# The first two projection chunks of a layer, walked by token halves over eight weight loads

## The chip, the cores and the metric

The kernel runs on one core of a Trainium2 chip. The metric is the device time of one execution in microseconds (us); it is the median of three timed runs. All times inside an execution are read from one profiled run, in us from the start of its span.

## What is computed

The reference is a two-layer decoder trunk over 256 tokens of width 2048. The part that matters here is the start of each layer: a row norm with a gain, and one wide projection whose output columns feed everything behind it.

```
def rms_norm(x, g):
    x32 = x.astype(jnp.float32)
    y = x32 * lax.rsqrt(jnp.mean(x32 * x32, axis=-1, keepdims=True) + EPS)
    return (y * g.astype(jnp.float32)).astype(x.dtype)
...
    u = rms_norm(h, norm_mix_pre)
    proj = u @ w_in
    offsets = tuple(int(o) for o in np.cumsum(IN_SIZES)[:-1])
    (nsa_q, nsa_kv, nsa_g, lru_x, lru_y,
     gla_q, gla_k, gla_v, gla_r, gla_z) = jnp.split(proj, offsets, axis=-1)
```

## The kernel before

Every matrix product is made of split operands: a value is the sum of a rounded part (`hi`, made by a ScalarE cast) and a rest (`lo`, a VectorE subtraction), and three matmuls (hi by hi, hi by lo, lo by hi) give one product. The helper `split` (L147 and L148) makes both parts, for the activations `u` and for every weight tile.

**Weights** come as a list of loads, in the order in which the projections use them (`plan`). `ensure` (L203 on) issues the next load from SyncE into one of four `raw` buffers and records its split into one of eight `hi`/`lo` buffers. A load therefore waits until VectorE has finished the split of the load four places ahead of it, and a split waits until TensorE has finished with the tile eight places ahead. All loads leave from SP's one queue, in the order of the program, and each waits for the load eight places ahead of it to land.

**The first two chunks of a layer** are `vw` (256 columns, four loads of 512 KB, four row blocks each) and `vs` (eight loads of 256 KB, two row blocks each). The tile of a `vs` load has 320 columns: 256 come with the load, the other 64 are gate columns, which lie elsewhere in `w_in`. These 64 are fetched once per layer for all eight tiles by two extra loads (`self.gz`, in `ensure`): 16 and 48 columns for each of 2048 rows, so runs of 64 and 192 bytes. Each `vs` tile then needs a second small split, out of that fetched tile. A `vs` matmul reads all 320 columns.

The 256 tokens are two halves of 128 (`hf`), because the stationary operand holds 128 tokens. Before, `form_a` ran `vw` with all its four loads for half 0 and then for half 1 (`grp=4`), and then `vs` load by load, both halves of each load in turn (`grp=1`). Each chunk has one accumulator per half, and `evac` copies it out behind the last matmul.

**The operand `u`** of the first layer is made in `run`: per half, ScalarE squares the four tiles of `h` with a running sum, VectorE and GpSimd turn that into a row factor, ScalarE scales each tile by it (L163) and VectorE multiplies by the gain (L151). `to_t` then transposes each tile on TensorE (L311) and splits the result. For the second layer the same is done at the end of the first layer, in `ev_pg` and `pre_norm`.

Other loads at the start: the input `x` in eight tiles `h`, the gain in two halves, the constants `cst`, two 512 KB loads of `nsa_cmp_w` (runs of 256 bytes) and nine small ones into `rows` (`load_params`). The order on each engine is set by a scheduler that works on the recorded program; it moves instructions ahead of others where it finds room.

Of the kernel before, what the change touches and what calls it, by code (L numbers as in the profile page):

```python
# [13 lines left out]
AF = mybir.ActivationFunctionType  # L14
ALU = mybir.AluOpType
# [16 lines left out]
NBUF = 8  # L32
# [68 lines left out]
class Trunk:  # L101
# [129 lines left out]
    def form_a(self, base, nu, k0, ut, evac, grp=1, kpu=2, w=512, ring=None):  # L231
        accs = [(ring or self.acc)() for _ in range(2)]
        self.ensure(base)
        for g in range(0, nu, grp):
            us = range(g, min(nu, g + grp))
            for hf in range(2):
                for u in us:
                    self.ensure(base + u)
                    hi, lo = self.loaded[base + u]
                    for k in range(kpu):  # L240
                        kt = k0 + kpu * u + k
                        uh, ul = ut.get(kt, hf * 128, hf * 128 + 128)
                        wh, wl = hi[:, k * w:k * w + w], lo[:, k * w:k * w + w]
                        last = u == nu - 1 and k == kpu - 1
                        o = accs[hf][:, 0:w]
                        self.mm(o, uh, wh, u == 0 and k == 0, False)
                        self.mm(o, uh, wl, False, False)
                        self.mm(o, ul, wh, False, last)
                    if hf:
                        self.ensure(base + u + NBUF)  # L250
                    self.pump(0.72 * kpu * w / 1024)
                if g + grp >= nu:
                    evac(hf, accs[hf])

    def banks(self, which):

        if which == "acc":
            return [self.acc() for _ in range(4)]
        return [self.sc(), self.sc(), self.tr(), self.tr()]
# [176 lines left out]
    def layer(self, i, ut):  # L436
        nc, a = self.nc, self.a
        B = lambda *k: self.base[(i,) + k]
# [5 lines left out]

        v = self.unit().rearrange("p (h b n) -> p h b n", h=2, b=2)

        self.form_a(B("vw"), 4, 0, ut, lambda hf, acc: nc.scalar.copy(v[:, hf, 1], acc[:, 0:256]), 4, 4, 256)
        gt = self.st([P, 2, 48], "gt", 1)
        z = self.sm(32)

# [2 lines left out]
            nc.vector.tensor_copy(z[:, hf * 16:hf * 16 + 16], acc[:, 256:272])  # L453
            self.actf(gt[:, hf], acc[:, 272:320], AF.Tanh, scale=0.5)
        rows = self.load_params(i)
        self.form_a(B("vs"), 8, 0, ut, ev_vs, 1, 2, 320)
        self.ts(gt, gt, 0.5, 0.5)
        gtv = self.st([P, 2, 16], "gtv", 1)
        self.tt(gtv, gt.rearrange("p h (n b) -> p h n b", b=3)[:, :, :, 0],
# [18 lines left out]
        for _ in range(2):  # L478
            t = self.unit(F32R)
            kh.append(t.rearrange("p (g b t) -> p g b t", g=2, b=2))  # L480
            t = self.unit(F32R)
# [101 lines left out]
        gpre = self.gain("norm_mlp_pre", i)  # L583
# [96 lines left out]
        last = i == self.depth - 1  # L680
        ss = [self.sm(4) for _ in range(2)]
        if not last:
            gpre = self.gain("norm_mix_pre", i + 1)
# [422 lines left out]
    def run(self):  # L1106
        self.plan()
        a = self.a
        self.h = [[self.sb.tile([P, 512], F32, name=f"h{hf}{n}") for n in range(4)] for hf in range(2)]
        ut = self.new_ut()  # L1110
        for hf in range(2):
            for n in range(4):
                self.dma(self.h[hf][n], a["x"][0, hf * 128:hf * 128 + 128, n * 512:n * 512 + 512])
            if hf == 0:
                gpre = self.gain("norm_mix_pre", 0)
                self.ensure(1)
            ss = self.sm(4)
            with self.tc.high_priority():
                for n in range(4):
                    self.sumsq(self.h[hf][n], ss[:, n:n + 1])  # L1120
                self.nrm[hf] = self.st([P, 4], "nrm", 4)
                r = self.rstd(ss, keep=self.nrm[hf])
                for n in range(4):
                    t = self.t2()
                    self.actf(t, self.h[hf][n], AF.Copy, scale=r)
                    self.tt(t, t, self.col(gpre, n))
                    self.to_t(t, n, hf, ut)
        self.cst2()
        for i in range(self.depth):
            ut = self.layer(i, ut)  # L1130
# [33 lines left out]
```

## Time and profile before

| | |
|---|---|
| median of three runs | 2487.36 us (2486.42 to 2487.51) |
| profiled execution | 2485.96 us |
| its span, first to last instruction | 2484.2 us, so 1.76 us lie around it |
| TensorE (PE) busy | 2458.3 us, 99% of the span |
| VectorE (DVE) busy | 1527.9 us, 62% |
| ScalarE (ACT) busy | 1279.2 us, 51% |
| mean granted TensorE clock | 0.997 |

The busy share of PE counts the time in which a matmul is under way; the chain that ended last tells what the end of the program waited for, step by step. A timeline row gives the start of a group of equal instructions, its time, and in brackets how long the engine was idle before it and what ended that. PE, DVE, ACT and SPq (the DMA issues of SyncE) have rows of their own, and L166 and L147/L148 are lines of helpers, so the names of the tiles tell which step a row belongs to.

### The profile page before, as it was taken

How to read it: one execution, taken by the hardware profiler on the slowest of the kernel's cores; microseconds unless marked ns; L12 is line 12 of the kernel's file. 1: busy time of each engine (PE TensorE's matmuls, PEld its weight loads, DVE VectorE, ACT ScalarE, POOL GpSimd, SP SyncE). 2: the span in 40 equal slices, each digit the busy share in tenths (PEclk: the TensorE clock that was granted, in tenths of full speed). 3: DMA queues.
4: the chain of work that ended last, by engine and by line, in shares of the span. 5: the costliest groups of instructions: out<-in, count | busy, mean ns of one | idle time of the engine just before them, and what ended most of it. 6: DMA issues, size and time to landing. Idle time of an engine off the chain costs nothing.

```text
span 2484.2 us, 33780 instructions
## 1 busy us (share of the span) xinstructions
PE 2458.3 (99%) x12950; PEld 2079.8 (84%) x12950; DVE 1527.9 (62%) x2098; ACT 1279.2 (51%) x2008; POOL 27.6 (1%) x42
## 2 busy tenths in 40 slices
PE   8999999999999999999999999999999999999999
PEld 7888888888888888888888888888888888888887
DVE  5776767754555554656667767676545546555574
ACT  6676655554443443445456765654544434444452
POOL 0000000000000000000000000000000000000000
PEclk9999999999999999999999999999999999999999
DMA  8644445556656556665575445456566565565653
GB/s 255 196 136 136 150 161 195 184 189 193 191 189 196 189 187 195 189 208 186 188 196 166 130 144 155 161 181 201 189 194 188 190 194 191 188 195 187 210 182 125
DMA packets 286371, 452.20 MB, mean 182 GB/s; under 512 B 32984, under 2 KB 107744, under 8 KB 286208
## 3 DMA queue, kind: packets, MB, share of 16 engines
q1 hardware_dynamic: 286208, 450.03, 56.9%
q8 instruction: 102, 1.67, 0.3%
q14 instruction: 61, 0.50, 0.1%
HBM read 447.88 MB, written 2.10 MB: 181 GB/s over the span
## 4 chain that ended last, share of the span: by engine, by line
PE 93%; DVE 3%; ACT 1%; DMA 1%; issue 1%; POOL 0%; DVEq 0%; ACTq 0%; SPq 0%; POOLq 0%
PE acc L166 62%; PE tr L166 14%; PE sc L166 14%; PE tr L873 1%; DMA raw<-in_w_up_dram 1%; DVE lo L148 1%; ACT t L163 1%; ACT hi L147 0%; PE tr L311 0%; DVE h L154 0%; DVE t L154 0%; DVE u L148 0%; DVE u L151 0%; POOL sm L301 0%; DVE u L154 0%
## 5 line engine op out<-in xcount | busy, mean ns | idle before, releaser
L148 DVE TENSOR_TENSOR lo<-raw,hi 128x1024 fp32r<-128x1024 f32 (+1 forms) x832 | 1007.2, 1213 | 789.9 <-ACT hi L147 784.8
L147 ACT CAST hi<-raw 128x1024 fp32r<-128x1024 f32 (+1 forms) x832 | 865.9, 1043 | 982.1 <-PE acc L166 571.8
L166 PE MATMUL acc<-hi,u 128*128 128x512 f32 (+2 forms) x2944 | 900.4, 384 | 3.7 <-DVE u L148 1.4
L166 PEld LDWEIGHTS acc<-hi,u 128*128 128x128 f32 x2944 | 547.2, 189 | 109.9 <-ACT u L147 2.5
L166 PE MATMUL acc<-lo,u 128*128 128x512 f32 (+2 forms) x1472 | 563.8, 383 | 0.9 <-DVE lo L148 0.9
L166 PE MATMUL acc<-u,hi 128*128 128x512 f32 x1920 | 490.2, 395 | 0.0
L166 PEld LDWEIGHTS acc<-u,hi 128*128 128x128 f32 x1920 | 344.6, 189 | 65.5 <-issue 3.1
L166 PEld LDWEIGHTS acc<-lo,u 128*128 128x128 f32 x1472 | 277.6, 189 | 52.4 <-DVE lo L148 1.4
L166 PEld LDWEIGHTS acc<-u,lo 128*128 128x128 f32 x1920 | 262.0, 190 | 18.9
L166 PE MATMUL acc<-u,lo 128*128 128x256 f32 x1920 | 268.2, 282 | 0.0
L166 PE MATMUL sc<-u,hi 128*128 128x512 f32 x512 | 140.3, 394 | 0.0
L166 PE MATMUL tr<-u,hi 128*128 128x512 f32 x512 | 138.4, 391 | 0.0
L166 PE MATMUL sc<-hi,u 128*128 128x512 f32 x384 | 119.3, 389 | 0.0
L166 PE MATMUL tr<-hi,u 128*128 128x512 f32 x384 | 119.2, 389 | 0.0
L166 PEld LDWEIGHTS tr<-u,hi 128*128 128x128 f32 x512 | 95.6, 188 | 21.5 <-issue 0.8
L166 PEld LDWEIGHTS sc<-u,hi 128*128 128x128 f32 x512 | 88.5, 190 | 11.8
L166 PEld LDWEIGHTS sc<-u,lo 128*128 128x128 f32 x512 | 78.3, 189 | 10.0
L166 PEld LDWEIGHTS tr<-hi,u 128*128 128x128 f32 x384 | 72.1, 188 | 14.9
L166 PEld LDWEIGHTS sc<-hi,u 128*128 128x128 f32 x384 | 72.1, 188 | 14.8
L166 PE MATMUL tr<-u,lo 128*128 128x256 f32 x512 | 82.9, 283 | 0.0
L166 PE MATMUL sc<-u,lo 128*128 128x256 f32 x512 | 81.3, 282 | 0.0
L166 PE MATMUL sc<-lo,u 128*128 128x512 f32 x192 | 74.8, 389 | 0.0
(185 smaller groups left out, 1705.6 us busy)
## 6 DMA issues: line engine op xcount, KB each, us to landing
raw<-in_w_up_dram SPq DMA_DIRECT2D x256, 512.0 KB, 3.7
raw<-in_w_down_dram SPq DMA_DIRECT2D x256, 512.0 KB, 3.5
raw<-in_w_in_dram SPq DMA_DIRECT2D x168, 512.0 KB, 3.7
raw<-in_w_out_dram SPq DMA_DIRECT2D x64, 512.0 KB, 3.6
raw<-in_w_ple_gate_dram SPq DMA_DIRECT2D x64, 512.0 KB, 4.1
raw<-in_w_in_dram SPq DMA_DIRECT2D x16, 256.0 KB, 3.0
raw<-in_w_ple_dram SPq DMA_DIRECT2D x8, 512.0 KB, 3.4
h<-in_x_dram SPq DMA_DIRECT2D x8, 256.0 KB
```

Of the source, the lines that this page charges most:

```text
L147: self.nc.scalar.copy(hi, src)
L148: self.nc.vector.tensor_sub(lo, src, hi.bitcast(F32))
L163: self.nc.scalar.activation(out, a, f, **k)
L166: self.nc.tensor.matmul(out, l, r, start=start, stop=stop, skip_group_check=True)
L873: nc.tensor.transpose(b[:, x * 128:x * 128 + 128], pe[:, x * 128:x * 128 + 128], self.ident)
```

## The change

The body of `form_a`'s innermost loop becomes a function of its own, `a_unit`. In `layer`, the two calls of `form_a` for `vw` and `vs` are replaced by one loop: first half 0 over the four `vw` loads and the first four `vs` loads, then half 1 over the same eight, then half 0 and half 1 over the last four `vs` loads. Four accumulators are taken at once. `load_params` now stands ahead of both chunks. In `run`, the scaling on ScalarE and the gain product on VectorE become one VectorE instruction, `stt` (L154, scalar_tensor_tensor).

```diff
@@ form_a @@
             for hf in range(2):
                 for u in us:
-                    self.ensure(base + u)
-                    hi, lo = self.loaded[base + u]
...
-                    if hf:
-                        self.ensure(base + u + NBUF)
-                    self.pump(0.72 * kpu * w / 1024)
+                    self.a_unit(base, u, nu, kpu, w, k0, ut, hf, accs[hf])
                 if g + grp >= nu:
                     evac(hf, accs[hf])
+
+    def a_unit(self, base, u, nu, kpu, w, k0, ut, hf, acc):
+        self.ensure(base + u)
+        hi, lo = self.loaded[base + u]
+        o = acc[:, 0:w]
+        for k in range(kpu):
+            kt = k0 + kpu * u + k
+            uh, ul = ut.get(kt, hf * 128, hf * 128 + 128)
+            wh, wl = hi[:, k * w:k * w + w], lo[:, k * w:k * w + w]
+            last = u == nu - 1 and k == kpu - 1
+            self.mm(o, uh, wh, u == 0 and k == 0, False)
+            self.mm(o, uh, wl, False, False)
+            self.mm(o, ul, wh, False, last)
+        if hf:
+            self.ensure(base + u + NBUF)
+        self.pump(0.72 * kpu * w / 1024)
@@ layer @@
-        self.form_a(B("vw"), 4, 0, ut, lambda hf, acc: nc.scalar.copy(v[:, hf, 1], acc[:, 0:256]), 4, 4, 256)
...
         rows = self.load_params(i)
-        self.form_a(B("vs"), 8, 0, ut, ev_vs, 1, 2, 320)
+
+        jobs = []
+        for key, nu, kpu, w, ev in (("vw", 4, 4, 256, lambda hf, acc: nc.scalar.copy(v[:, hf, 1], acc[:, 0:256])),
+                                    ("vs", 8, 2, 320, ev_vs)):
+            jobs.append((B(key), nu, kpu, w, ev, [self.acc() for _ in range(2)]))
+        self.ensure(B("vw"))
+        for part in ((0, 0, 4), (1, 0, 4)), ((1, 4, 8),):
+            for hf in range(2):
+                for x, u0, u1 in part:
+                    base, nu, kpu, w, ev, accs = jobs[x]
+                    for u in range(u0, u1):
+                        self.a_unit(base, u, nu, kpu, w, 0, ut, hf, accs[hf])
+                    if u1 == nu:
+                        ev(hf, accs[hf])
@@ run @@
                     t = self.t2()
-                    self.actf(t, self.h[hf][n], AF.Copy, scale=r)
-                    self.tt(t, t, self.col(gpre, n))
+                    self.stt(t, self.h[hf][n], r, self.col(gpre, n), op0=ALU.mult, op1=ALU.mult)
                     self.to_t(t, n, hf, ut)
```

Beyond the starts of the two layers the order of the instructions is the same on every engine. Three places show what moved.

SP's queue in the first layer, behind the fourteen loads that both kernels begin with (`raw_268` and `raw_286` are the last two `vw` loads, `raw_317` on are `vs` loads, `u_321` is the tile of the gate columns). Before:

```order
L144 DMA raw_268<-in_w_in_dram 128x4x256 [waits DMAHW6_49]
L144 DMA raw_286<-in_w_in_dram 128x4x256 [waits DMAHW7_49]
L144 DMA raw_317<-in_w_in_dram 128x2x256 [waits DMAHW0_49,DVE_49]
L144 DMA raw_328<-in_w_in_dram 128x2x256 [waits DMAHW1_49,DVE_49]
L144 DMA rows_423<-in_lru_conv_w_dram 16x128 [waits DMAHW2_49]
L144 DMA rows_423<-in_lru_conv_b_dram 4x128 [waits DMAHW3_49]
L144 DMA rows_423<-in_lru_ba_dram 4x128 [waits DMAHW4_49]
L144 DMA u_237<-in_nsa_cmp_w_dram 128x16x64 [waits DMAHW5_49]
L144 DMA u_238<-in_nsa_cmp_w_dram 128x16x64 [waits DMAHW6_49]
L144 DMA u_321<-in_w_in_dram 128x16x16 [waits DMAHW7_49]
L144 DMA u_321<-in_w_in_dram 128x16x48 [waits DMAHW0_49]
L144 DMA raw_336<-in_w_in_dram 128x2x256 [waits DMAHW1_49,DVE_49]
```

Now, behind the same fourteen and nine `rows` loads (`raw_274` and `raw_292` are the last two `vw` loads, `raw_311` on are `vs` loads, `u_315` takes the gate columns; DMAHW0 to DMAHW7 are the eight places of which each load waits for its own, DVE is a wait for a split):

```order
L144 DMA raw_274<-in_w_in_dram 128x4x256 [waits DMAHW7_49]
L144 DMA u_229<-in_nsa_cmp_w_dram 128x16x64 [waits DMAHW0_49]
L144 DMA u_230<-in_nsa_cmp_w_dram 128x16x64 [waits DMAHW1_49]
L144 DMA raw_292<-in_w_in_dram 128x4x256 [waits DMAHW2_49]
L144 DMA raw_311<-in_w_in_dram 128x2x256 [waits DMAHW3_49,DVE_49]
L144 DMA raw_328<-in_w_in_dram 128x2x256 [waits DMAHW4_49,DVE_49]
L144 DMA raw_342<-in_w_in_dram 128x2x256 [waits DMAHW7_49,DMAHW5_49,DVE_49]
L144 DMA raw_356<-in_w_in_dram 128x2x256 [waits DMAHW6_49,DMAHW2_49,DVE_49]
L144 DMA raw_382<-in_w_in_dram 128x2x256 [waits DMAHW3_49,DVE_49]
L144 DMA raw_402<-in_w_in_dram 128x2x256 [waits DMAHW4_49,DMAHW0_49,DVE_49]
L144 DMA u_315<-in_w_in_dram 128x16x16 [waits DMAHW1_49]
L144 DMA u_315<-in_w_in_dram 128x16x48
```

All nine `rows` loads and both `nsa_cmp_w` loads now stand ahead of the fourth `vw` load, and the gate columns stand behind six `vs` loads instead of two, four of which wait for splits of this stage.

PE's queue where `vs` begins in the first layer. Before (`acc_243` is `vw` for half 1, `acc_433` and `acc_434` are `vs` for half 0 and half 1):

```order
L166 MATMUL acc_243<-lo_288,u_85 128x256
L166 MATMUL acc_243<-hi_287,u_85 128x256
L166 MATMUL acc_433<-hi_318,u_78 128x320 [waits Activation_49]
L166 MATMUL acc_434<-hi_318,u_78 128x320
L166 MATMUL acc_433<-lo_319,u_78 128x320 [waits DVE_49]
```

Now (`acc_246` is `vw` for half 0, `acc_248` is `vs` for half 0):

```order
L166 MATMUL acc_246<-lo_294,u_85 128x256
L166 MATMUL acc_246<-hi_293,u_85 128x256
L166 MATMUL acc_248<-hi_312,u_78 128x320 [waits Activation_49]
L166 MATMUL acc_248<-lo_313,u_78 128x320 [waits DVE_49]
L166 MATMUL acc_248<-hi_312,u_78 128x320 x2
L166 MATMUL acc_248<-lo_313,u_78 128x320
```

Half 1 of `vw`, 48 matmuls, stood ahead of the first `vs` matmul and now stands behind the 24 matmuls of half 0 over four `vs` loads.

PE's queue in the second layer behind the last transposes (`tr`). Before (`acc_10866` is `vw` for half 1):

```order
L311 MATMUL tr_10851<-ident,u_10110 128x128 [waits DVE_49,PE_49]
L311 MATMUL tr_10851<-ident,u_10110 128x128 x3
L166 MATMUL acc_10866<-lo_10633,u_10111 128x256
L166 MATMUL acc_10866<-hi_10632,u_10111 128x256
L166 MATMUL acc_10866<-hi_10632,u_10112 128x256 [waits Activation_49]
```

Now (`acc_10871` is `vs` for half 0, `acc_10870` is `vw` for half 1):

```order
L314 MATMUL tr_10843<-ident,u_10102 128x128 [waits DVE_49,PE_49]
L314 MATMUL tr_10843<-ident,u_10102 128x128 x3
L166 MATMUL acc_10871<-hi_10748,u_10103 128x320 [waits Activation_49]
L166 MATMUL acc_10870<-hi_10624,u_10103 128x256
L166 MATMUL acc_10870<-lo_10625,u_10103 128x256
L166 MATMUL acc_10871<-lo_10749,u_10103 128x320 [waits DVE_49]
```

The `vs` matmuls of half 0 now follow the last transposes at once; SP's queue of the second layer is unchanged.

## Rows read from the trace of the kernel before

**Rows 1.** The page: busy time by engine, and the chain that ended last by engine.

```profile
PE 2458.3 (99%) x12950; PEld 2079.8 (84%) x12950; DVE 1527.9 (62%) x2098; ACT 1279.2 (51%) x2008; POOL 27.6 (1%) x42
...
PE 93%; DVE 3%; ACT 1%; DMA 1%; issue 1%; POOL 0%; DVEq 0%; ACTq 0%; SPq 0%; POOLq 0%
```

**Rows 2.** Windows: stretch; busy us (instructions) of PE, PEld, DVE, ACT, POOL; PEclk; DMA share; GB/s.

```profile
10.40:20.70 10.30, 8.31 (x34) 7.38 (x35) 7.43 (x15) 8.90 (x21) 1.71 (x4) 0.50 1.08 365
20.70:34.40 13.70, 12.10 (x96) 11.20 (x94) 9.15 (x18) 7.83 (x19) 1.48 (x2) 1.00 0.93 197
34.90:49.30 14.40, 14.30 (x97) 14.27 (x98) 9.18 (x18) 8.69 (x19) 0.00 (x0) 1.00 0.73 224
```

**Rows 3.** Timeline of PE, first layer: transposes, vw matmuls (128x256), first vs matmuls (128x320).

```profile
10.81 1.97 PE L311 MATMUL tr<-ident,t 128*128 128x128 f32 x8 [4.33 <-DVE t L151]
13.95 0.58 PE L166 MATMUL acc<-hi,u 128*128 128x256 f32 x1 [1.17 <-ACT u L147]
...
18.17 0.41 PE L166 MATMUL acc<-lo,u 128*128 128x256 f32 x1
...
18.81 0.41 PE L166 MATMUL acc<-lo,u 128*128 128x256 f32 x1
...
30.10 0.40 PE L166 MATMUL acc<-hi,u 128*128 128x256 f32 x2
...
30.46 0.40 PE L166 MATMUL acc<-hi,u 128*128 128x256 f32 x2
...
35.00 0.56 PE L166 MATMUL acc<-hi,u 128*128 128x320 f32 x2 [0.66 <-ACT hi L147]
```

**Rows 4.** Timeline of SP's DMA issues, first layer.

```profile
9.75 0.33 SPq L144 DMA_DIRECT2D cst<-in_cst_dram  x1
11.09 5.68 SPq L144 DMA_DIRECT2D raw<-in_w_in_dram  x4
...
18.03 4.12 SPq L144 DMA_DIRECT2D u<-in_nsa_cmp_w_dram  x2
22.20 4.53 SPq L144 DMA_DIRECT2D u<-in_w_in_dram  x2
```

**Rows 5.** DMA issues of the whole run: KB each, median us from issue to landing.

```profile
raw<-in_w_in_dram SPq DMA_DIRECT2D x168, 512.0 KB, 3.7
...
u<-in_nsa_cmp_w_dram SPq DMA_DIRECT2D x4, 512.0 KB, 5.7
...
u<-in_w_in_dram SPq DMA_DIRECT2D x2, 384.0 KB, 5.3
```

**Rows 6.** Timelines of ACT, then DVE, first layer: weight splits, vw evacuation, gate casts.

```profile
22.14 1.05 ACT L147 CAST hi<-raw 128x1024 fp32r<-128x1024 f32 x1
...
34.38 0.37 ACT L447 COPY u<-acc 128x256 f32<-128x256 f32 x1 [4.28 <-PE acc L166]
34.65 0.70 ACT L147 CAST hi<-u 128x128 fp32r<-128x128 f32 x3
...
23.22 1.23 DVE L148 TENSOR_TENSOR lo<-raw,hi 128x1024 fp32r<-128x1024 f32 x1
...
28.34 0.68 DVE L148 TENSOR_TENSOR lo<-raw,hi 128x512 fp32r<-128x512 f32 x1
```

**Rows 7.** Timelines: the row scaling on ACT; one scalar_tensor_tensor of the same size on DVE.

```profile
9.31 2.56 ACT L163 ACTIVATE t<-h,nrm 128x512 f32<-128x512 f32 x4 [1.12 <-POOL nrm L301]
...
1242.93 0.69 DVE L154 SCALAR_TENSOR_TENSOR t<-t,u 128x512 f32<-128x512 f32 x1 [3.72 <-ACT t L163]
```

**Rows 8.** Timelines of PE, ACT, DVE, second layer: last transposes, first gate casts and subtractions.

```profile
1261.35 0.60 PE L311 MATMUL tr<-ident,u 128*128 128x128 f32 x4
...
1262.25 0.30 ACT L147 CAST hi<-u 128x128 fp32r<-128x128 f32 x1
...
1262.73 0.28 DVE L148 TENSOR_TENSOR lo<-u,hi 128x128 fp32r<-128x128 f32 x1
...
1263.59 0.68 DVE L148 TENSOR_TENSOR lo<-u,hi 128x128 fp32r<-128x128 f32 x3
```

More of the change, by code (lines that the diff above doesn't have):

```diff
@@ L237, in form_a @@
                 for u in us:
-                    self.ensure(base + u)
-                    hi, lo = self.loaded[base + u]
[L240 to L248, printed above, removed]
-                    if hf:
-                        self.ensure(base + u + NBUF)
-                    self.pump(0.72 * kpu * w / 1024)
+                    self.a_unit(base, u, nu, kpu, w, k0, ut, hf, accs[hf])
                 if g + grp >= nu:
                     evac(hf, accs[hf])
+    def a_unit(self, base, u, nu, kpu, w, k0, ut, hf, acc):
[13 more added lines that the diff above has]
+        self.pump(0.72 * kpu * w / 1024)
     def banks(self, which):
```

## The prediction

> **What bounds the kernel now.** I read the page first. TensorE is busy for 99% of the span and carries 93% of the chain that ended last [rows 1]: whatever makes PE wait, or gives back a wait, moves the end one for one, and work of the other engines counts only where PE waits for it. Only two places change, the starts of the two layers, so the windows and the timeline of PE there come next. The reader should see three things in them. PE runs its first `vw` matmul at 13.95 and its first `vs` matmul at 35.00 [rows 3]; between 20.70 and 34.40 it is idle for only 13.70 − 12.10 = 1.6 us, and through `vs`, from 34.90 to 49.30, hardly at all: 97 matmuls in 14.3 us, 0.147 us each [rows 2]. The granted clock was 0.50, the 1.2 GHz level, from about 10.4 to 20.7, behind 4.33 us in which PE had nothing to do [rows 2, 3]. And the loads of this stretch run at 365 GB/s [rows 2], so here the order of SP's queue decides when PE can go on. Therefore SP's issues and the times to landing are the third view [rows 4, 5].
>
> The gate columns are the load to watch. Before, SP issues them at 22.20, in 4.53 us [rows 4], and ACT casts them at 34.65, just behind the evacuation at 34.38 that waited for PE [rows 6]: at that time they had long been there, and PE lost 0.66 us [rows 3].
>
> **The change, part by part.** All 96 `vw` and 96 `vs` matmuls remain, with the same shapes. What changes is what must be ready before which of them.
>
> *Row scaling.* Eight ACT instructions go (four in 2.56 us, 0.64 each), and eight VectorE products become eight scalar_tensor_tensors, 0.69 each by a row of the same size [rows 7]. The transposes start some 0.3 to 0.7 us earlier per half. Cover: PE then still waits for the weights. If that cover were gone, the gain would be 0.7 us. I count 0.
>
> *The first `vs` matmul, first layer.* It needs its tile's gate columns, and PE's queue is in order, so everything behind waits too: the other `vs` matmuls and all 48 `vw` matmuls of half 1. I call its start T; before it is 35.00. At full clock three 128x256 matmuls take 0.36 us (30.10 to 30.46), 0.120 each [rows 3], so the 48 matmuls that now stand behind T are 5.8 us. The end of the stage moves by (T − 35.00) + 5.8. T = 29.2 would be no change.
>
> T follows down SP's queue:
> 1. The `cst` load is issued at 9.75 [rows 4], when the first gain half has landed. Still to land then are the second gain half (512 KB), two weight loads (1024), four tiles of x (1024) and `cst` itself (417): 3.05 MB at 365 GB/s [rows 2], 8.3 us, so 18.1. The eighth of the nine small loads waits for `cst`, the ninth and the third `vw` load wait for small loads just behind it; at about 0.4 us an issue the third `vw` load leaves at 18.9, not at 11.09 [rows 4].
> 2. With 3.7 us to landing [rows 5] it is there at 22.6. Its cast ran at 22.14 before [rows 6], so this alone costs nothing.
> 3. Two `nsa_cmp_w` loads are in front of the fourth `vw` load. 512 KB at 365 GB/s are 1.44 us. Runs of 256 bytes took 2.0 us longer to landing than a weight load of the same size (5.7 against 3.7 [rows 5]); so each holds the queue between 1.44 us and 3.4 us. I take the middle, 2.4. The fourth `vw` load lands at 22.6 + 2 x 2.4 + 1.44 = 28.8.
> 4. Its split is 1.05 us on ACT and 1.23 us on DVE [rows 6]: 31.1. Half 0 of `vw` is then finished after another 11 matmuls, at 32.4.
> 5. That split frees the buffer of the fourth `vs` load; the fifth and sixth wait for the next two splits, 0.6 us each (0.68 with the overlap of neighbours [rows 6]). The sixth leaves at 32.3, the two gate loads at 32.7 and 33.2.
> 6. The larger one lands 5.3 us later [rows 5], at 38.5, and the first cast takes 0.30 [rows 8]: T = 38.8.
>
> So the stage ends 3.8 + 5.8 = **9.6 us** later. Bounds: with 1.44 us per `nsa_cmp_w` load and the gate load at the 3.7 us of a weight load, T = 35.3 and the cost is 6.1; with 3.4 us, and SP held on the short-run loads as it was before (4.12 and 4.53 us for two issues [rows 4]), T = 42 and the cost is 13.
>
> [...] The trace has 5.3 us for the 384 KB of gate columns and 5.7 us for 512 KB in runs of 256 bytes [rows 5]. [...]
>
> *The clock.* PE is idle from 32.4 to 38.8, 6.4 us, longer than the 4.33 us that stood ahead of the low stretch [rows 3]. I expect the clock at 1.2 GHz when `vs` begins. There three matmuls took 0.64 us (18.17 to 18.81), 0.213 each, against 0.120 [rows 3]. Before, PE ran matmuls from 13.95 until the clock rose at 20.7 [rows 2, 3]: 6.75 us that did the work of 3.8, a loss of 2.95. Now the matmuls come without gaps, which speaks for a shorter stretch. Bounds: 0, and 4.5 for the whole 10.3 us at half rate. I take **2.5**, near that row.
>
> *Second layer.* SP's queue is unchanged there and the gate columns are in time, but the first `vs` matmul now follows the last transposes, which PE ends at about 1261.8 [rows 8], or 0.4 sooner since four matmuls no longer stand before them. It waits for the cast (1262.25 + 0.30), its `lo` partner for the subtraction (1262.73 + 0.28), and the second tile's for one of the three from 1263.59 on [rows 8]. PE loses 1.1 + 0.2 + 0.1 less what the chain gains: **1.2 us**, bounds 0.5 and 2.
>
> *The rest.* The last four `vs` tiles wait for weight buffers that half 1 of `vw` frees; a tile's split is under 1 us on each engine [rows 6], against 1.8 us of PE per tile (12 x 0.147). The cover is thick, and if it were gone, one split, 1.5 us, would show. The `rows` loads come earlier, but nothing before the third chunk needs them.
>
> Sum: 9.6 + 2.5 + 1.2 − 0 = 13.3 us on the profiled execution's 2485.96, 2499.3. The median is 1.4 us above that execution, so 2500.7; I forecast 2500.5.
>
> **The rivals.**
> - *The clock does not fall*, or is back at once. For it: the trace has a single fall of this sort, and PE has a burst of work in between. 2500.7 − 2.5 = 2498. Chance 0.22.
> - *Short runs cost no more than long ones.* Then the queue drains at 1.44 us per 512 KB and the gate load lands after 3.7: T = 35.3, 6.1 + 1.2 without a fall of the clock, 2494.7. [...] Chance 0.07.
> - *Not slower: the gate columns are not what PE waits for.* If they land before half 0 of `vw` is finished, T is 32.4 and only 3.2 us are lost; if the fourth `vw` load also comes 3 us sooner, because the small loads let SP go before `cst` is there, T is near 29.2, where nothing is lost, and below that the earlier start of half 0 begins to pay. 2487 to 2491.5. Against it stands the order of the queue: the gate loads leave behind a split of the fourth `vw` load. Chance 0.10.
> - *Worse: SP is held.* Long issues like 4.12 and 4.53 us [rows 4] ahead of the gate loads, and the long low clock: 13 + 3 + 1.5, 2505. Chance 0.11.
>
> **How the numbers follow.** The forecast has 0.50. A measurement of this kernel can tell about 0.2%, 5 us, from no change: the limits are 2482.4 and 2492.3. Only the third rival lies below the upper one; faster by over 5 us would need more than the 1.6 us of idle time and the 2.95 us of lost clock of this stage together, so 0.02; within 0.2%, 0.09; slower, 0.89. The range runs from the second rival's time, less 1.7 for a second layer without loss, to the fourth: 2493 to 2505; it leaves out the third rival and half of the fourth, 0.15.
>
> **What would show it.** In the profile after: the third `vw` load issued near 18.9 and the gate loads near 33; PE idle for some 6 us before its first 128x320 matmul near 38.8, released by ACT's cast of the gate columns, which in turn waited for their DMA; a granted clock below 1 around 36 to 44; in the second layer about 1 us of PE idle behind the last transposes; the scalar_tensor_tensors near 0.69 us each. I am wrong in size if T lies elsewhere, and in kind if PE goes from `vw` to `vs` without a stop or the gate casts did not wait for their load.

## The result and the profile after

The changed kernel takes 2507.69 us in the median of six runs, against 2487.44 for the kernel before beside it: a ratio of 1.0081, 95% interval 1.007 to 1.0091, so 20.2 us slower. The direction was forecast and the size was not: 13.3 us, with a range that ended at 2505.

The page of the changed kernel, the lines that answer to [rows 1]:

```profile
PE 2462.6 (98%) x12950; PEld 2082.5 (83%) x12950; DVE 1529.7 (61%) x2098; ACT 1275.3 (51%) x2000; POOL 27.6 (1%) x42
...
PE 91%; DVE 3%; DMA 2%; ACT 2%; issue 1%; POOL 0%; SPq 0%; ACTq 0%; DVEq 0%; POOLq 0%
```

PE's share of the last chain fell from 93% to 91%; what came in are DMA and ACT. PE is busy 4.3 us longer with the same 12950 matmuls; the stretches of low clock below account for 3.5 of that. The rest of the 20.2 is idle time.

**Where the 20.2 us lie.** One instruction stands at the same place of PE's program in both kernels, behind the chunks c0 and c1: the transpose of the row parameters, once per layer. The timeline of PE of the kernel before, then of the changed kernel:

```profile
71.76 0.25 PE L408 MATMUL tr<-ident,rows 100*128 100x100 f32 x1
...
1303.77 0.25 PE L408 MATMUL tr<-ident,rows 100*128 100x100 f32 x1
```

```profile
39.70 0.64 PE L166 MATMUL acc<-hi,u 128*128 128x320 f32 x1 [6.96 <-ACT hi L147]
...
61.48 0.27 PE L480 MATMUL tr<-ident,sm 128*16 128x128 f32 x1
...
66.67 0.28 PE L480 MATMUL tr<-ident,sm 128*16 128x128 f32 x1 [2.73 <-DVE sm L455]
...
67.37 3.40 PE L166 MATMUL acc<-u,hi 128*128 128x512 f32 x8
...
71.73 1.99 PE L166 MATMUL acc<-u,hi 128*128 128x512 f32 x8
...
88.48 0.25 PE L411 MATMUL tr<-ident,rows 100*128 100x100 f32 x1
...
1279.03 0.54 PE L166 MATMUL acc<-hi,u 128*128 128x320 f32 x2 [0.66 <-ACT hi L147]
...
1303.56 0.28 PE L480 MATMUL tr<-ident,sm 128*16 128x128 f32 x1 [2.07 <-DVE sm L455]
...
1323.80 0.25 PE L411 MATMUL tr<-ident,rows 100*128 100x100 f32 x1
```

The first mark is 88.48 − 71.76 = 16.7 us later, the second 20.0, the end of the span 20.2. So the first layer's start costs 16.7 and the second's 3.3. Within the first layer:

- The first `vs` matmul starts at 39.70, not at 35.00 [rows 3]: 4.7, and the 48 moved matmuls are 5.8. Together 10.5.
- From there to the first transpose of the gate columns (L480) are 21.78 us. 96 matmuls of 0.147 and 48 of 0.120 are 19.9. The other 1.9 us are the low clock behind the stop.
- The second of these transposes waits 2.73 us for a VectorE copy. Behind it eight 128x512 matmuls take 3.40 us instead of 1.99, and the next eight are back to that: a second low stretch, about 1.6 us with the matmuls around it.

10.5 + 1.9 + 2.7 + 1.6 = 16.7. The windows of the changed kernel show both stretches of low clock (columns as in [rows 2]): 0.57 and 0.53 over the stop and the first 17 matmuls behind it, then 1.00, and 0.66 behind the second wait:

```profile
32.50:39.60 7.10, 0.24 (x3) 0.04 (x1) 1.11 (x2) 1.24 (x4) 0.00 (x0) 0.57 0.95 218
39.60:44.00 4.40, 4.30 (x17) 4.26 (x18) 0.90 (x4) 0.64 (x4) 0.00 (x0) 0.53 0.17 59
44.00:58.00 14.00, 14.00 (x107) 14.00 (x106) 6.07 (x11) 6.61 (x12) 0.00 (x0) 1.00 0.58 181
66.67:71.70 5.03, 5.03 (x22) 4.33 (x23) 2.77 (x4) 2.44 (x5) 0.00 (x0) 0.66 0.93 294
```

The waits of PE by releaser (us in all, times, longest) name the same two places. The first line was 1.0 in all before, and the second did not exist:

```profile
PE acc L166 <- ACT hi L147: 9.1, 4, 7.0
...
PE tr L480 <- DVE sm L455: 4.8, 2, 2.7
```

**The chain to the first stop** ran as forecast. SP's issues in the changed kernel, where the third `vw` load is the single one at 18.54 and the gate columns are at 32.76:

```profile
18.54 0.42 SPq L144 DMA_DIRECT2D raw<-in_w_in_dram  x1
19.01 3.25 SPq L144 DMA_DIRECT2D u<-in_nsa_cmp_w_dram  x2
22.31 10.40 SPq L144 DMA_DIRECT2D raw<-in_w_in_dram  x7
32.76 3.26 SPq L144 DMA_DIRECT2D u<-in_w_in_dram  x2
```

ACT's rows: the fourth `vw` load's cast at 28.80, the cast of a part of `u` ahead of it, the evacuation of `vw` half 0, and the gate casts, which waited for their DMA:

```profile
28.53 0.37 ACT L147 CAST u<-tr 128x256 fp32r<-128x256 f32 x1 [1.41 <-DVE u L148]
28.80 2.76 ACT L147 CAST hi<-raw 128x1024 fp32r<-128x1024 f32 x4
32.78 0.37 ACT L460 COPY u<-acc 128x256 f32<-128x256 f32 x1 [1.22 <-PE acc L166]
...
39.35 0.90 ACT L147 CAST hi<-u 128x128 fp32r<-128x128 f32 x4 [4.79 <-DMA u<-in_w_in_dram]
```

**The chain to the second stop** was not in the forecast. The copy of half 1's gate columns out of its accumulator (L455) runs at 66.44, though the accumulator was finished at 61.6. On DVE it stands behind three weight splits of c1, and it also waits for ACT's evacuation (L454), which stands behind three casts of c1. The last of those waited for its load. ACT, then DVE:

```profile
64.22 1.04 ACT L147 CAST hi<-raw 128x1024 fp32r<-128x1024 f32 x1 [1.14 <-DMA raw<-in_w_in_dram]
65.17 0.37 ACT L454 COPY u<-acc 128x256 f32<-128x256 f32 x1
```

```profile
65.30 1.23 DVE L148 TENSOR_TENSOR lo<-raw,hi 128x1024 fp32r<-128x1024 f32 x1 [0.95 <-ACT hi L147]
66.44 0.17 DVE L455 COPY sm<-acc 128x16 f32<-128x16 f32 x1
```

PE's queue has matmuls of c0 behind the transpose. Their weights had been split by 60.6, but they could not pass it.

In the kernel before, the same evacuation and copy (L452, L453) stand behind casts and splits of c0 and ahead of all of c1, and the two transposes run without a wait. ACT, DVE, then PE:

```profile
49.85 0.37 ACT L452 COPY u<-acc 128x256 f32<-128x256 f32 x1
```

```profile
51.03 0.17 DVE L453 COPY sm<-acc 128x16 f32<-128x16 f32 x1
```

```profile
49.90 0.27 PE L465 MATMUL tr<-ident,sm 128*16 128x128 f32 x1
...
51.52 0.27 PE L465 MATMUL tr<-ident,sm 128*16 128x128 f32 x1
```

### The profile page after: what moved, and what is told of

It reads as the page before. It is cut to its first block, busy times and chain, and to the rows that moved or that the text cites. A ratio compares the mean times of both kernels' runs of the same rounds, so it can differ in the third digit from the quotient of the medians.

```text
span 2504.4 us, 33774 instructions
## 1 busy us (share of the span) xinstructions
PE 2462.6 (98%) x12950; PEld 2082.5 (83%) x12950; DVE 1529.7 (61%) x2098; ACT 1275.3 (51%) x2000; POOL 27.6 (1%) x42
## 4 chain that ended last, share of the span: by engine, by line
PE 91%; DVE 3%; DMA 2%; ACT 2%; issue 1%; POOL 0%; SPq 0%; ACTq 0%; DVEq 0%; POOLq 0%
PE acc L166 61%; PE tr L166 14%; PE sc L166 14%; DMA raw<-in_w_in_dram 1%; DVE lo L148 1%; PE tr L888 1%; DMA raw<-in_w_up_dram 1%; ACT hi L147 1%; DVE u L148 1%; ACT t L163 0%; PE tr L314 0%; DVE t L154 0%; DVE h L154 0%; DVE u L151 0%; POOL sm L304 0%
## 5 line engine op out<-in xcount | busy, mean ns | idle before, releaser
L147 ACT CAST u<-tr 128x256 fp32r<-128x256 f32 (+1 forms) x124 | 46.0, 382 | 59.7 <-PE tr L314 22.7
```

The costliest lines, as they stand in the source:

```text
L147: self.nc.scalar.copy(hi, src)
```

## The experiments

Theory: three separate costs. The gate columns leave behind loads that wait for splits (T); PE then stands a second time, in both layers, behind the gate transposes; the clock falls behind such stops. Rivals: the new VectorE instruction costs something; the loads of `vs`, c0 and c1 are late themselves, so that a wait taken away only moves; going by halves starves PE of buffers, whatever the loads do.

Each run is compared with runs of the kernel before on the same chip. The marks are the two transposes of the row parameters in the profiled execution: the start of the first, and the distance to the second.

| run | median us | ratio to before (95%) | first mark | distance |
|---|---|---|---|---|
| before | 2487.2 to 2487.8 | 1 | 71.76 | 1232.0 |
| after | 2507.69 | 1.0081 (1.007 to 1.0091) | 88.48 | 1235.3 |
| e1 | 2487.63 | 0.9998 (0.9989 to 1.0007) | 72.30 | 1231.7 |
| e2 | 2510.99 | 1.0091 (1.0077 to 1.0105) | 88.64 | 1235.5 |
| e3 | 2494.50 | 1.0029 (1.0017 to 1.004) | 79.34 | 1231.4 |
| e4 | 2500.23 | 1.0049 (1.0037 to 1.0062) | 83.04 | 1232.7 |
| e5 | 2499.43 | 1.0041 (1.0028 to 1.0053) | 81.07 | 1235.9 |
| e6 | 2498.43 | 1.0042 (1.0029 to 1.0054) | 76.78 | 1241.2 |
| e7 | 2489.48 | 1.0008 (0.9999 to 1.0017) | 77.71 | 1229.9 |
| e8 | 2485.85 | 0.9992 (0.9983 to 1.0001) | 72.38 | 1230.6 |
| e9 | 2507.47 | 1.008 (1.0068 to 1.0093) | 86.26 | 1235.8 |
| e10 | 2501.94 | 1.006 (1.0047 to 1.0072) | 86.48 | 1234.5 |
| e11 | 2492.45 | 1.0025 (1.0015 to 1.0034) | 72.45 | 1239.1 |
| e12 | 2482.76 | 0.9979 (0.997 to 0.9988) | 70.38 | 1230.0 |

**e1 and e2: the two parts of the change, each alone.**

```diff
@@ run, in the kernel before (e1); the reverse, in the changed kernel (e2) @@
-                    self.actf(t, self.h[hf][n], AF.Copy, scale=r)
-                    self.tt(t, t, self.col(gpre, n))
+                    self.stt(t, self.h[hf][n], r, self.col(gpre, n), op0=ALU.mult, op1=ALU.mult)
```

> The kernel before with the one VectorE instruction for row scaling and norm product, and nothing else of the change. My theory: PE waits for the weights in this stretch, not for the scaled tiles, so the time is that of the kernel before, 2487.4, within 2 us, and the first 128x320 matmul starts within 0.7 us of 35.00. Rival, the new instruction carries part of the loss because it lengthens VectorE's part of the start: 3 us or more above the kernel before.

> The changed kernel with the row scaling on ScalarE and the product on VectorE as before, so the new order of chunks and loads alone. My theory: the whole loss is the order's, so 2507.7 within 2 us, with the gate loads issued near 33 and PE idle near 7 us before its first 128x320 matmul. Rival, the new instruction carries part of the loss: 2504 or less.

The new instruction alone changes nothing that can be measured. The order alone costs all of it: 2511 (four runs from 2506.9 to 2513.6), a little above the bound of my theory and far from the rival's 2504. Whether the instruction saves the 3.3 us by which the changed kernel is below that is not shown: the intervals overlap. One detail of e1 went outside its bound: the first 128x320 matmul came 1.6 us earlier, at 33.43, but PE stood later for the gate transposes, 1.05 and 0.56 us, and the first mark is no earlier than before. So small waits at these transposes come with the old order too.

**e3: the gate loads behind the fourth `vw` load.**

```diff
@@ layer @@
-        self.ensure(B("vw"))
+        self.ensure(B("vw") + 3)
+        self.gates(i)
@@ ensure: the two loads of self.gz go into gates() @@
```

In this kernel the second layer's splits read the gate columns of the first layer's tile, because `ensure` runs ahead of `layer`; the first layer is complete.

> The changed kernel with the two loads of the gate columns moved six places forward in SP's queue, right behind the fourth vw load and ahead of the first vs load. My theory: PE waited 7 us for these columns and for nothing else; issued near 23 instead of 32.8 they land near 32, the first 128x320 matmul starts near 34 instead of 39.7, the granted clock stays at 1 there, and the time falls by 5.7 + 1.8 = 7.5 us to 2500 (2498 to 2503). Rival, the six vs loads are as late, so that PE waits for their splits instead: the time falls by less than 2 us.

SP's issue of the gate columns and PE's rows:

```profile
24.91 3.91 SPq L144 DMA_DIRECT2D u<-in_w_in_dram  x2
```

```profile
35.47 0.46 PE L166 MATMUL acc<-hi,u 128*128 128x320 f32 x2
...
59.07 0.28 PE L481 MATMUL tr<-ident,sm 128*16 128x128 f32 x1 [1.96 <-DVE sm L455]
...
79.34 0.25 PE L411 MATMUL tr<-ident,rows 100*128 100x100 f32 x1
```

The stop of 6.96 us is gone: PE enters `vs` without a wait, 4.2 us earlier than in the changed kernel and not 5.7. The clock did not stay up, though. It was low again from 24.2, behind a wait of 2.01 us ahead of transposes of `u`, and so through nearly all matmuls of the last two `vw` loads for half 0 (a window with columns as in [rows 2]; e5 and e7 have the same from about 26 to 36):

```profile
24.20:34.40 10.20, 8.42 (x35) 6.97 (x34) 5.70 (x12) 5.51 (x12) 0.53 (x1) 0.50 1.10 244
```

The first mark comes 9.1 us earlier, not 7.5, as the second gate transpose waited 0.8 us less and the clock did not fall behind that wait (1.6). The whole gained 13.2; the other 4 us lie between the marks. The rival falls: no other wait took the place of this one.

**e4: the gate transposes behind c0 and c1.** The block of the two transposes and the copy `gzt` moves behind the loop over c0 and c1, with `z` as its input as before.

```diff
@@ layer @@
-        for hf in range(2):
-            nc.tensor.transpose(b[0:16, hf * 128:hf * 128 + 128], z[:, hf * 16:hf * 16 + 16], self.ident)
-        nc.scalar.copy(gzt, b[0:16, 0:T])
...
         for x in range(2):
             self.form_b(B("c", x), 4, ut, None, dst=kcu[:, x * 512:x * 512 + 512])
+        for hf in range(2):
+            nc.tensor.transpose(b[0:16, hf * 128:hf * 128 + 128], z[:, hf * 16:hf * 16 + 16], self.ident)
+        nc.scalar.copy(gzt, b[0:16, 0:T])
```

> The changed kernel with the two transposes of the gate columns and their copy moved behind the next two chunks (c0 and c1); loads, splits and their order on VectorE stay. My theory: PE stood 2.73 us in the first layer and 2.07 us in the second for the copy of the gate columns, which VectorE had queued behind weight splits of c1, while matmuls of c0 were ready behind the transpose; both waits go, and with the first the low clock behind it (about 1.6 us), so the time falls by 6.4 us to 2501.3 (2500 to 2503.5). Rival, the weights of c0 and c1 themselves are late, and the wait only moves into their matmuls: the time falls by less than 2 us.

It gained 7.5 us, a little more than forecast. PE still stops at its first `vs` matmul, and then has no wait up to the mark in the first layer:

```profile
39.11 0.64 PE L166 MATMUL acc<-hi,u 128*128 128x320 f32 x1 [5.39 <-ACT hi L147]
...
82.82 0.38 PE L486 MATMUL tr<-ident,sm 128*16 128x128 f32 x2
```

So the weights of c0 and c1 were not what PE lacked. They were late only for engines that had to take them in order, ahead of the copy.

**e5: as e3, with each layer's own gate columns**, fetched in `ensure` right behind the load of the fourth `vw` tile.

> The loads of the gate columns right behind the fourth vw load, as in the run before that moved them (e3), but for each layer with its own columns. My theory, from that run: the first layer is 9 us shorter (its first 128x320 matmul near 34.6), and the start of the second layer 4 us, because with the gate columns cast early the scheduler puts vs matmuls of half 0 ahead of the last transposes, where PE waited; 2494.5 (2493 to 2497). Rival, the gain in the second layer came from splits that did not wait for the second layer's own columns: 2498.5.

2499.4, near the rival, but its five runs go from 2492.6 to 2501.0, so the time does not decide. The traces say more: from the second layer's first transposes of `u` that had to wait (1258.78) to its first gate transpose (1290.23) PE takes 31.45 us, as in e3 (1255.54 to 1287.00), against 34.99 in the changed kernel (1264.05 to 1299.04). So this part of the gain is there with the layer's own columns too. The profiled execution differs from e3 in two things:

```profile
59.24 0.28 PE L482 MATMUL tr<-ident,sm 128*16 128x128 f32 x1 [1.88 <-DVE sm L457]
...
81.07 0.25 PE L413 MATMUL tr<-ident,rows 100*128 100x100 f32 x1
...
1295.12 0.28 PE L482 MATMUL tr<-ident,sm 128*16 128x128 f32 x1 [2.44 <-DVE sm L457]
...
1316.94 0.25 PE L413 MATMUL tr<-ident,rows 100*128 100x100 f32 x1
```

Between the transpose and the mark lie 21.83 and 21.82 us, against 20.27 in e3: the clock fell behind both waits, 1.57 us each. The wait in the second layer was 2.44, against 1.06. Why these differ from e3 is not settled.

**e6: `load_params` behind both chunks**, which gives SP back nearly its old order while PE keeps the new one.

> The changed kernel with load_params moved behind both chunks, so that SP's queue of the first layer is again nearly that of the kernel before (third and fourth vw load right behind cst, the gate loads ahead of the third vs load), while PE keeps the new order by halves. My theory: what cost time was the order of the loads, not the order of the matmuls; the first 128x320 matmul starts near 30.5 instead of 39.7, which with the 48 matmuls behind it is only 1.3 us later than before, the clock does not fall there, and what is left are the waits for the copies of the gate columns (2 + 2 us) and the second layer's 1.2: 2494 (2491 to 2497). Rival, going by halves itself starves PE of buffers (the last four vs tiles and c0 are behind half 1 of vw): 2500 or more.

2498.4, between the two: 9.3 us gained, 11 left. PE's rows:

```profile
31.26 0.42 PE L166 MATMUL acc<-hi,u 128*128 128x320 f32 x1 [0.93 <-ACT hi L147]
...
56.53 0.28 PE L480 MATMUL tr<-ident,sm 128*16 128x128 f32 x1 [2.55 <-DVE sm L455]
...
76.78 0.25 PE L411 MATMUL tr<-ident,rows 100*128 100x100 f32 x1
...
1296.12 0.28 PE L480 MATMUL tr<-ident,sm 128*16 128x128 f32 x1 [3.01 <-DVE sm L455]
```

The long stop is gone, and the first mark comes 11.7 us earlier. The waits at the gate transposes stay, 2.55 and 3.01, though the loads of the first layer now leave early. So waits of this size belong to the order by halves. 5.0 us are left at the first mark. Between the marks this execution loses 9.2, and not all of that is the order's: three stretches of low clock lie there. The first is in a part of the first layer that the change does not touch:

```profile
133.60:136.90 3.30, 3.30 (x14) 2.93 (x13) 1.61 (x4) 1.56 (x3) 0.00 (x0) 0.50 0.41 114
```

The second, from 1263.4 to 1266.7, is behind a wait of 1.42 us that the kernel before has as well, the third behind the wait of 3.01. Such stretches turn up in single executions (see the last section), so the distance in one execution is good to 2 or 3 us, not better. The profiles of the kernel before and of the changed kernel have none that lies outside the places of the change.

**e7: both mends (e5 and e4).**

> Gate loads right behind the fourth vw load and the two transposes of the gate columns behind c0 and c1, both together. My theory: both waits are separate, so the waits for the copies that were left with the early gate loads (1.96 and 1.06 us) go as well: 2491.5 (2489.5 to 2493.5). Rival, they overlap (the copies were late only because the gate columns were): no less than 2494.

2489.5, at the lower end of the forecast: 18.2 of the 20.2 us are back. Neither pair of gate transposes waits any more:

```profile
77.49 0.38 PE L488 MATMUL tr<-ident,sm 128*16 128x128 f32 x2
...
1307.34 0.38 PE L488 MATMUL tr<-ident,sm 128*16 128x128 f32 x2
```

The two waits are separate costs: e5 alone gained 8.3 us, e4 alone 7.5, both together 18.2.

**e8: the small loads late as well** (`load_params` and the `nsa_cmp_w` loads behind both chunks, on top of e7).

> As the one with early gate loads and late transposes, and with load_params and the two nsa_cmp_w loads moved behind both chunks as well, so that nothing but weights and the gate columns stands in SP's queue. My theory: the fourth vw load lands near 17 instead of 28.7, PE then waits only for the transposed halves of u, the first 128x320 matmul starts near 29, and the time is that of the kernel before or a little better, 2486 (2483 to 2488). Rival, the loads that were put off are late for compress or the row parameters, and PE waits there: 2490 or more.

2485.9, as forecast: with only weights and the gate columns in SP's queue, and the gate transposes late, the kernel with the order by halves is no slower than the kernel before (1.9 us below it, with an interval that reaches 1). The first `vs` matmul starts at 29.80, where I had expected it near 29.

**e9: the copies ahead of one c1 split.** The scheduler is told that the evacuation is urgent.

```diff
@@ layer @@
-                        ev(hf, accs[hf])
+                        with self.tc.high_priority():
+                            ev(hf, accs[hf])
```

> The changed kernel with the evacuation of vs marked urgent for the scheduler; on VectorE the copy of the gate columns of half 1 then stands behind two weight splits of c1 instead of three, and nothing else moves ahead of the transposes. My theory: the wait was the place of that copy in VectorE's queue, behind a split whose weights had not landed; the copy runs when the second split ends, some 0.5 us after PE gets there, so the waits of 2.73 and 2.07 us shrink to 0.7 or less and the time falls by 4 to 5.5 us to about 2503 (2501 to 2504.5). Rival, the accumulator or ScalarE's evacuation sets the time of the copy: 2506 or more.

No gain, as the rival said. ACT, DVE and PE of this kernel:

```profile
64.31 0.36 ACT L454 COPY u<-acc 128x256 f32<-128x256 f32 x1
```

```profile
64.71 0.17 DVE L455 COPY sm<-acc 128x16 f32<-128x16 f32 x1 [0.89 <-ACT u L454]
```

```profile
64.94 0.28 PE L481 MATMUL tr<-ident,sm 128*16 128x128 f32 x1 [2.45 <-DVE sm L455]
```

One place nearer on DVE, the copy waited 0.89 us for ACT's evacuation, which still stood behind the third cast of c1; and the scheduler had put the transpose ahead of six more matmuls of c0. So the copy did come sooner, 3.6 us behind the first gate transpose instead of 5.0, but PE came to its transpose 1.0 us sooner and still waited 2.45. Both queues hold the copy, not DVE's alone; what the place on DVE alone is worth, this run does not show.

**e10 and e11: the order by halves in one layer only** (`if i == 0` or `if i == 1` around the new loop, the two old calls of `form_a` otherwise).

> The new order by halves in the first layer alone, the second layer as before. My theory, from the two traces: of the 20.2 us, 16.7 are lost ahead of the row parameters' transposes of the first layer and 3.6 at the start of the second, so 2487.6 + 16.7 = 2504.3 (2502.5 to 2506). Rival, the second layer costs only the 1.2 us that I forecast, and the rest of its 3.6 was a chance of that execution: 2506.5.

> The new order by halves in the second layer alone, with the new row scaling; the first layer otherwise as before. My theory: 3.6 us, of which 2.07 are the wait for the copy of the gate columns and the rest the gate casts behind the last transposes: 2491.2 (2490 to 2494, the upper end if the clock falls behind the wait). Rival: the 1.2 us of my forecast, 2488.8.

14.7 us for the first layer, a little below my range, and 5.2 us for the second, inside it. The rival for the second layer, 1.2 us, falls. Together 19.9 of the 20.2. In the profiled execution of e11 the second gate transpose waits longer than the 2.07 us of the changed kernel, and the clock falls behind it:

```profile
1289.90 0.38 PE L485 MATMUL tr<-ident,sm 128*16 128x128 f32 x1 [3.18 <-DVE sm L455]
```

**e12: the order by halves in the second layer only, with both mends.**

> The order by halves in the second layer alone, with the gate loads one place earlier and the transposes of the gate columns behind c0 and c1, and the new row scaling in the first layer. My theory: the second layer then takes the 54.0 us between its first and last transposes that the two runs with both mends showed (56.1 before), and the first layer is that of the kernel before: 2485.5 (2484 to 2487). Rival, the gate loads one place earlier hold back the first layer's vs loads: 2488 or more.

2482.76, ratio 0.9979 (0.997 to 0.9988): 4.5 us faster than the kernel before, and the best of all. PE's marks:

```profile
70.38 0.25 PE L413 MATMUL tr<-ident,rows 100*128 100x100 f32 x1
...
1300.35 0.25 PE L413 MATMUL tr<-ident,rows 100*128 100x100 f32 x1
```

The first comes 1.4 us earlier than before, where the late gate transposes help too, and the distance is 2.0 us shorter. Set beside e8, with the same mends and the order by halves in both layers, the first mark is 2.0 us earlier (70.38 and 72.38): in the first layer the old order looks like the better one. No run has the mends with the old order in both layers, so how much of the 4.5 us is the order's in the second layer is not shown.

## Why the prediction was wrong in size

- *What bounds the kernel*: right. All 20.2 us lie at the starts of the two layers, as waits of PE or slow matmuls behind them.
- *Row scaling, 0*: right (e1). The instruction takes 0.74 us, and 0.69 from one to the next in a row of four, as forecast.
- *T, steps 1 to 6*: right in the main. The third `vw` load left at 18.54 (forecast 18.9), the fourth was cast at 28.80 (28.8), half 0 of `vw` was evacuated at 32.78 (32.4), the gate loads left at 32.76 (32.7), T was 39.70 (38.8), so 10.5 us instead of 9.6. The cast at 28.80 agrees in part by luck: I had the load land at 28.8 and the cast begin then, but the cast stood behind ACT's cast of `u` at 28.53, which waited 1.41 us for VectorE, so the load may have been there earlier. The gate columns were there 6.6 us after their first issue (32.76 to 39.35), where my steps had 5.8. e3 shows that this wait was a cause of its own: without it `vs` began 4.2 us earlier and the first mark came 9.1 us earlier, 2.3 of which belong to the second wait and the clock behind it.
- *The clock, 2.5*: the fall behind the stop cost 1.9, within its bounds. I had argued for a shorter stretch than the one before. It was as long, with the clock at 1.2 GHz from 33.5 to 43.7, and cost less because PE had nothing to run until 39.70. The rival without a fall did not come.
- *Second layer, 1.2*: its mechanism was right (3.3 less the 2.07 of the wait at the gate transposes leaves 1.2), but it was little more than a third of what that layer lost in the profiled execution; e11 measured 5.2 in the median.
- *The rest, 0*: **this step failed.** I wrote that the last four `vs` tiles wait for buffers, that "the cover is thick", and that otherwise one split would show. For the `vs` matmuls that held: PE did not wait for them. But I stopped there. The casts of those four tiles could start only as half 1 of `vw` freed their buffers, from 46.84 on; the loads of c0 leave as these splits end, and those of c1 as the splits of c0 end. For PE they were not late: the first load of c0 left 13.3 us ahead of its first matmul (at 48.21), in the kernel before 9.6 us ahead (at 39.62). But three casts and splits of c1 now stood ahead of the evacuation of `vs` half 1 on ACT and DVE, the third of them waiting for its load, where before there were only those of c0. PE in turn had the second gate transpose ahead of ready c0 matmuls. That is 2.73 + 2.07 us of waits and one more fall of the clock, 1.57: 6.4 us in the profiled execution, and 7.5 us by e4. Without it the kernel takes 2500.2 (e4), against the 2500.5 forecast. The terms that I did price came to 10.5 + 1.9 + 1.2 = 13.6, against 13.3; that they agree so well is partly luck, since T was 0.9 too low and the clock 0.6 too high.

The rows that could have warned are those of the transposes and copies in the kernel before. The second transpose ran at 51.52 without a wait, but its copy at 51.03 had ended only 0.3 us earlier. In the new order the first transpose stands right behind the last `vs` matmul (before, behind three matmuls of c0) and the second behind eleven matmuls of c0, as before: its place on PE did not change, the queues that feed it did. I priced the loads of this stretch but not the engine queues behind it. The fourth rival came nearest in size, 2505, for a wrong reason: the fourth `vw` load and the gate loads left when I had said.

## What to carry to other kernels

When an order is changed, follow the moved work one stage further than the change: the queues of the engines that are off the critical path are filled in another order there, and a small copy that comes to stand behind work that waits for a load can stop the bottleneck. A transpose or a small matmul that needs such a copy belongs behind work that is ready, not at the first place where it fits (7.5 us here, e4). Extra loads that feed every tile of a chunk (here the gate columns) go ahead of the loads that wait for buffers (8.3 us here, e5).

## What the runs showed that I had not expected

The clock does not fall after every stop of the same length. From the second gate transpose to the mark lie about 20.25 us with the clock at 2.4 GHz throughout, and 21.68 to 21.83 with a stretch at 1.2 GHz. It fell behind waits of 1.88 and 2.44 (e5), 2.73 (the changed kernel, first layer), 3.01 (e6) and 3.18 us (e11), and not behind waits of 1.06 and 1.96 (e3), 1.78 and 2.65 (e2), 2.07 (the changed kernel, second layer), 2.41 (e10) and 2.55 (e6). (e9 is left out: its transpose has other matmuls between it and the mark.) So the length of the wait alone did not decide in this band, and each place of this kind carries an uncertain 1.57 us.

Nor are these the only places. At the start of the second layer nine of the kernels have a wait of PE of 1.42 or 1.43 us for a split of `u`, ahead of a `vw` matmul; behind it the clock fell in e6 and e10 and stayed up in the other seven. And in e6, e8, e10 and e11 it was low for a stretch between 129 and 147, where PE had waited no longer than 0.26 us: two rows of PE that lie 19.76 us apart in the kernel before (125.93 and 145.69) lie 21.29 apart in e6 (130.93 and 152.22). So differences of about 1.5 us in the distance between the marks need not come from the change: e10 has 2.5 more than the kernel before, with the old order in the second layer.

The runs of e5 and e6 spread by 8.4 and 6.6 us, those of e7 and e8, without the waits, by 2.8 and 2.6. But e3 and e10 have such waits and spread by 3.9 and 3.3, and the kernel before spread by up to 6.0, so it is not shown that the waits make the spread.
